# A Strassen-Winograd MLP in a hybrid decoder step: the second layer's seven products in another order, with other first steps and longer load leads

## The chip, the cores and the metric

The kernel runs on one core of a Trainium2 chip. A core has five engines that work side by side, each on its own list of instructions and strictly in the order of that list: TensorE (PE, products), VectorE (DVE), ScalarE (ACT), GpSimd (POOL) and SyncE (SP, which here only issues DMAs). Engines wait for one another through semaphores. The metric is the device time of one execution in microseconds; lower is better.

## The reference

One step of a hybrid decoder layer: attention and a state-space mixer, then a squared-ReLU MLP between RMSNorms. The change touches the second product of the MLP alone and what stands at its two ends:

```python
def rmsnorm(x, g):
    xf = x.astype(jnp.float32)
    y = xf * lax.rsqrt(jnp.mean(xf * xf, axis=-1, keepdims=True) + EPS)
    return (y * g.astype(jnp.float32)).astype(x.dtype)
...
    u = jax.nn.relu(rmsnorm(h, norm2_g) @ w_up)
    return h + (u * u) @ w_down
```

A last rmsnorm gives y. The model width is 1024, the MLP's 4096; there are 1024 prompt positions (without the meta tokens) and 32 of the running samples, 1056 columns (TM) in all. Everything is float32.

## The kernel before

**Numbers.** Each float32 operand is split into a high part in fp32r (a cast on ACT) and a low part (a subtraction on DVE), and each product of blocks is made as three: high by high, high by low, low by high (`three`). For weights, `split_w` (L1194 to L1198) does this into six rooms, used in turn: two each of whi, wlo and a third name (w7x in the up layer, w7y in the down layer). A room is free again when PE has ended the step that used it.

**MLP by seven products.** Both layers cut their matrices in two halves each way and use the Strassen-Winograd scheme, in which seven products of half size take the place of eight. The columns' halves have 528 columns (TH), a quarter 264 (TQ). The up layer runs over 16 pairs p of output blocks and, for each, over products j in the order 5, 1, 2, 6, 7, 4, 3 (1 and 2 of the first six pairs are done ahead); a product is 24 matmuls of 128x264. `run_up` copies sums from PSUM on ACT (s, L1243), adds on DVE, applies relu and square, and POOL writes the seven activation sums that the down layer needs to DRAM, `u7[k]`, one array for each k (L1316, L1317; k is the pair that made it). A pair's weights come in two loads (`load_up`, L1206), each into one of two rooms.

**Down layer.** `ORDER` gives the order of its products; the first six run as `down`, 16 steps k each. `step_down` (L1375) does one step: 24 matmuls into eight PSUM banks (two named c, three g, three b), all sums of a scheme added up in the banks. At k = 15 DVE adds the eight banks to a quarter of the residual h (L1386); `INTO` says which. The next product cannot write a bank until that addition has read it. The activation of a step is loaded into `tr` (L1493, 264 KB), cast (L1495) and split (L1496) into `ts`. The weights come from loads of 256 KB (wdr), with sums in place for some products: product 5 takes S = x + z (L1505), product 3 x - (S - R) with R (`Rd`) loaded there (L1510, L1511), product 1 R, 6 the new S, 7 R - x (L1519), 4 a block as it is. Weights are made two steps ahead of their use.

**First steps.** So that PE need not stop between the layers, `EARLY` = 3 steps of product 5 are loaded, summed and split in rooms of the up layer during its last pair (`load_first`, `sum_first`, `split_first`). The other rooms of the down layer are only opened behind it.

**End.** Product 2 has its own loop, over quarters and half the output blocks, with its weights (w2, from `wdq`) and activations (`tsq`, `tk`, from `trq`) prepared three ahead. `final` makes the last norm of a quarter of the columns: squares on ACT (L1529), their sums on DVE (q, down to `ac`), a product with ones on PE to add across partitions, x to -1/2 on POOL (L311, `rs`), a diagonal matrix `dg` (L1547), a product of that with ones to spread it, and the scaling of h (L1556). It is written as a generator, and each `next` between steps lets it do one piece.

A scheduler may move independent instructions of an engine past one another; what it did is shown below, as lists of the built programs.

Of the kernel before, what the change touches and what calls it, by code (L numbers as in the profile page):

```python
# [191 lines left out]
def body(ctx: ExitStack, tc: tile.TileContext, xT, xm, win, wdt, wo, wu, wd, ck, cv, sc, st, sT, vec, consts,  # L192
# [1011 lines left out]
    def load_up(p, n, early):  # L1204
        r = (pu if n or early else wring).tile([128, 8, 128], F32, name=f"wraw{n}", tag="wraw2" if n or early else "wraw", bufs=2)
        SP.dma_start(out=r, in_=wu[p + 16 * n])  # L1206
        raws[p, n] = r

    def prep_up(p, j, first):

        if first:
# [4 lines left out]
        if (p, 1) in raws:
            a21, a22 = raws[p, 1][:, 0:4], raws[p, 1][:, 4:8]
        tt = DVE.tensor_tensor
        if j == 5:
            S_[p] = pu.tile([128, 4, 128], F32, name="S", tag="S", bufs=2)  # L1220
            tt(out=S_[p], in0=a21, in1=a22, op=ALU.add)
        elif j == 6:
            tt(out=S_[p], in0=S_[p], in1=a11, op=ALU.subtract)
        elif j == 7:
            tt(out=a21, in0=a11, in1=a21, op=ALU.subtract)
# [116 lines left out]
    def load_first(k, part):  # L1342

        if k < 2 and part == "z":
            early["r", k] = raw_tile()
            early["w", k] = early["r", k][:, 0:4], early["r", k][:, 4:8]
        elif k == 2:
            early["w", k] = early["r", 0][:, 4:8], early["r", 1][:, 4:8]
        if part == "a":
            early["a", k] = pu.tile([128, 2, TQ], F32, name="x5", tag="s3" if k == 2 else "s1", bufs=1 if k == 2 else 2).rearrange("p c t -> p (c t)")  # L1350
            SP.dma_start(out=early["a", k], in_=u7[k][:, SLOT[5]])
        else:
            SP.dma_start(out=early["w", k][0], in_=wd[k, :, 1])
            SP.dma_start(out=early["w", k][1], in_=wd[k + 16, :, 1])

    def sum_first(k):
        x, z = early["w", k]
        DVE.tensor_tensor(out=x, in0=x, in1=z, op=ALU.add)
        Sv[k] = flat(x)

    def split_first(k):
        if k != 1:
            early["t"] = pu.tile([128, 4, TH], F32R, name="t5", tag="u" if k else "x", bufs=2)
        t, a = early["t"][:, 2 * (k % 2):2 * (k % 2) + 2], early["a", k]
        w = split_w(pu, "w7x", early["w", k][0])
# [112 lines left out]
    sr_s = ctx.enter_context(ExitStack())
    srp = sr_s.enter_context(pool("srp", side="right"))
    R = srp.tile([128, 16, 512], F32, name="Rd")  # L1480
    S = srp.tile([128, 16, 512], F32, name="Sd")
# [8 lines left out]
    def acts(j, k, a=0, w=TH):  # L1490

        x = dn.tile([128, TH], F32, name="tr", tag="tr", bufs=3)[:, :w]
        SP.dma_start(out=x, in_=u7[k][:, SLOT[j], a:a + w])  # L1493
        t = dn.tile([128, 2, TH], F32R, name="ts", tag="ts", bufs=3)[:, :, :w]
        ACT.copy(out=t[:, 0], in_=x)  # L1495
        DVE.tensor_tensor(out=t[:, 1], in0=x, in1=f(t[:, 0]), op=ALU.subtract)  # L1496
        return t

    def weights_down(j, k):
        tt = DVE.tensor_tensor  # L1500
        s, r = Sv.get(k, S[:, k]), R[:, k]
        shaped = lambda a: a.rearrange("p (m q) -> p m q", m=4)
        if j == 5:
            x, z = block(k, 1, 0), block(k, 1, 1)
            tt(out=s, in0=flat(x), in1=flat(z), op=ALU.add)  # L1505
            return shaped(s)
        if j == 3:
            SP.dma_start(out=shaped(r), in_=wd[k, :, 0])
            x = block(k, 0, 1)
            tt(out=s, in0=s, in1=r, op=ALU.subtract)  # L1510
            tt(out=flat(x), in0=flat(x), in1=s, op=ALU.subtract)  # L1511
            return x
        if j == 1:
            return shaped(r)
        if j == 6:
            return shaped(s)
        if j == 7:
            x = block(k, 1, 0)
            tt(out=flat(x), in0=r, in1=flat(x), op=ALU.subtract)  # L1519
            return x  # L1520
        return block(k, 1 if j == 4 else 0, 1)
# [170 lines left out]
```

## Time and profile before

| | |
|---|---|
| median of 3 timed runs | 1173.1 us (1171.42 to 1176.45) |
| the profiled execution: time | 1180.33 us |
| its span | 1178.6 us |
| mean granted TensorE clock | 0.981 |
| down layer, first step of product 5 to last step of the step loop | 816.5 to 1107.4 us |

The profile is of one execution. "Idle before" in brackets is how long an engine stood still ahead of an instruction, with what released it. The page divides the span into 40 slices of 29.5 us; here are PE's and the DMA's busy tenths and the clock:

```profile
PE   8999989999999998999999999998899999999996
...
PEclk9999999999999999999999999999999999999898
DMA  8311110111466477656552534336999433665373
```

### The profile page before, as it was taken

What the parts mean: (1) busy time and instruction counts of PE and PEld (TensorE: products, weight loads), DVE (VectorE), ACT (ScalarE), POOL (GpSimd) and SP (SyncE); (2) the same over time, 40 slices, a digit from 0 to 9 for tenths busy, and PEclk for the clock granted to TensorE, in tenths of its full rate; (3) what the DMA queues carried; (4) which work ended last, traced back from release to release, by engine and by line L of the source; (5) the groups of instructions that cost most, each with busy time, mean ns of one, the idle gap of its engine ahead of it and who ended that gap; (6) DMA issues with size and microseconds to landing.
All of it is one profiled execution on the core that took longest, in us unless ns stands there. A gap on an engine that the chain in (4) does not pass through costs nothing.

```text
span 1178.6 us, 21734 instructions
## 1 busy us (share of the span) xinstructions
PE 1130.9 (96%) x8393; PEld 1088.9 (92%) x8393; DVE 840.2 (71%) x1634; ACT 558.3 (47%) x1176; POOL 240.1 (20%) x258
## 2 busy tenths in 40 slices
PE   8999989999999998999999999998899999999996
PEld 6899978889888897999999999998899999999996
DVE  7665888996689955988777777775687654746583
ACT  7312556665576646854434444443334333444351
POOL 4632343634435454210000000000000000000000
PEclk9999999999999999999999999999999999999898
DMA  8311110111466477656552534336999433665373
GB/s 286 112 37 37 37 37 18 37 38 53 132 209 202 128 233 224 200 181 225 189 182 106 180 117 154 147 120 220 317 289 295 135 93 94 181 183 148 114 238 102
DMA packets 87448, 177.64 MB, mean 151 GB/s; under 512 B 11028, under 2 KB 37556, under 8 KB 85296
## 3 DMA queue, kind: packets, MB, share of 16 engines
q1 hardware_dynamic: 80288, 141.44, 39.7%
q0 software_dynamic: 6224, 33.74, 7.1%
q8 instruction: 66, 1.08, 0.4%
q10 hardware_dynamic: 832, 1.07, 0.3%
q14 instruction: 38, 0.31, 0.1%
HBM read 125.49 MB, written 50.72 MB: 150 GB/s over the span
## 4 chain that ended last, share of the span: by engine, by line
PE 61%; DVE 14%; DMA 10%; issue 6%; ACT 4%; POOL 1%; SPq 1%; DVEq 0%; POOLq 0%; ACTq 0%
PE g L202 34%; PE b L202 14%; PE c L202 7%; PE s L202 2%; DMA wdr<-in_wd 2%; PE o L202 1%; DMA trq<-u 1%; DVE bc L512 1%; DVE p L638 1%; DMA hb<-hd 1%; DMA Rd<-in_wd 1%; DMA tr<-u 1%; DVE Qs L671 1%; DMA wdq<-in_wd 1%; DMA hb<-in_xm 1%
## 5 line engine op out<-in xcount | busy, mean ns | idle before, releaser
L202 PE MATMUL g<-acth,wlo 128*128 128x384 f32 (+2 forms) x624 | 193.9, 331 | 4.5 <-DVE hb L918 3.7
L202 PE MATMUL g<-acth,whi 128*128 128x384 f32 (+2 forms) x624 | 195.8, 335 | 1.5 <-DVE hb L918 1.4
L202 PE MATMUL g<-actl,whi 128*128 128x384 f32 (+2 forms) x528 | 175.1, 332 | 1.0 <-DVE actl L397 1.0
L1495 ACT CAST ts<-tr 128x528 fp32r<-128x528 f32 x93 | 58.9, 633 | 141.3 <-PE b L202 112.2
L202 PEld LDWEIGHTS g<-acth,wlo 128*128 128x128 f32 x624 | 117.5, 192 | 8.0 <-issue 3.5
L1496 DVE TENSOR_TENSOR ts<-tr,ts 128x528 fp32r<-128x528 f32 x93 | 65.6, 707 | 79.2 <-ACT ts L1495 79.1
L202 PEld LDWEIGHTS g<-acth,whi 128*128 128x128 f32 x624 | 116.7, 191 | 5.1 <-issue 3.6
L202 PEld LDWEIGHTS g<-actl,whi 128*128 128x128 f32 x528 | 101.1, 192 | 3.6 <-DVE actl L397 2.5
L311 POOL TENSOR_TENSOR rs<-rs,nhalf 128x3 f32<-128x3 f32 x10 | 11.1, 1114 | 347.3 <-DVE rs L310 347.3
L1243 ACT COPY s<-g 128x264 f32<-128x264 f32 x90 | 34.0, 379 | 71.4 <-PE g L202 70.2
L1248 DVE TENSOR_TENSOR u<-b,s 128x264 f32<-128x264 f32 x64 | 27.5, 431 | 26.5 <-PE b L202 14.8
L1316 POOL DMA_DIRECT2D u<-u x16 | 8.5, 532 | 180.9 <-ACT u L1259 149.1
L225 POOL TENSOR_TENSOR wlo<-wraw,whi 128x1024 fp32r<-128x1024 f32 (+1 forms) x18 | 41.9, 2328 | 16.3 <-ACT whi L224 16.2
L1253 ACT ACTIVATE u<-u 128x528 f32<-128x528 f32 x42 | 27.1, 646 | 28.6 <-DVE u L1252 28.6
L202 PE MATMUL g<-ts,w7y 128*128 128x264 f32 x279 | 40.1, 290 | 0.0
L202 PE MATMUL b<-ts,wlo 128*128 128x264 f32 x279 | 39.9, 289 | 0.0
L202 PE MATMUL g<-ts,wlo 128*128 128x264 f32 x279 | 39.7, 288 | 0.0
L202 PE MATMUL b<-ts,w7y 128*128 128x264 f32 x279 | 39.6, 287 | 0.0
L202 PE MATMUL g<-ts,whi 128*128 128x264 f32 x279 | 39.2, 285 | 0.0
L202 PE MATMUL b<-ts,whi 128*128 128x264 f32 x279 | 38.6, 283 | 0.0
L202 PEld LDWEIGHTS g<-ts,w7y 128*128 128x128 f32 x279 | 37.1, 193 | 0.0
L202 PEld LDWEIGHTS b<-ts,wlo 128*128 128x128 f32 x279 | 36.9, 193 | 0.0
(550 smaller groups left out, 3358.5 us busy)
## 6 DMA issues: line engine op xcount, KB each, us to landing
tr<-u SPq DMA_DIRECT2D x93, 264.0 KB, 2.8
wraw<-in_wu SPq DMA_DIRECT2D x38, 512.0 KB, 3.9
wdr<-in_wd SPq DMA_DIRECT2D x74, 256.0 KB, 4.4
u<-t POOLq DMA_DIRECT2D x16, 1056.0 KB, 5.5
wraw<-in_win SPq DMA_DIRECT2D x16, 512.0 KB, 3.7
u<-u POOLq DMA_DIRECT2D x10, 792.0 KB, 3.6
wraw<-in_wo SPq DMA_DIRECT2D x24, 256.0 KB, 3.2
h<-he SPq DMA_DIRECT2D x16, 264.0 KB, 4.4
```

Source lines behind the costliest of these rows:

```text
L202: PE.matmul(out, lhsT=a, rhs=b, start=start, stop=stop, skip_group_check=on)
L225: eng.tensor_tensor(out=lo[:, k], in0=raw[:, k], in1=f(hi[:, k]), op=ALU.subtract)
L311: POOL.tensor_tensor(out=out, in0=out, in1=nhalf[:out.shape[0], :w], op=ALU.pow)
L512: DVE.scalar_tensor_tensor(out=acc, in0=cb[:, j:j + CL], scalar=cw_(j), in1=acc, op0=ALU.mult, op1=ALU.add)
L638: DVE.tensor_tensor_reduce(out=s_out, in0=ps, in1=mask, scale=-scale, scalar=nsink, op0=ALU.add, op1=ALU.min, accum_out=nm)
L671: DVE.tensor_tensor(out=Q[oth, g, :, :rows], in0=src, in1=f(Q[own, g, :, :rows]), op=ALU.subtract)
L1243: ACT.copy(out=s[:, c], in_=ps[c][:, :TQ])
L1248: DVE.tensor_tensor(out=out[:, c], in0=ps[c][:, :TQ], in1=s[:, c], op=ALU.add)
L1253: ACT.activation(out=x, in_=x, func=AF.Square)
L1316: POOL.dma_start(out=u7[p][:, 4 + a:7], in_=u[:, a:3])
L1495: ACT.copy(out=t[:, 0], in_=x)
L1496: DVE.tensor_tensor(out=t[:, 1], in0=x, in1=f(t[:, 0]), op=ALU.subtract)
```

## The change

It does five things.

1. The first six products of the down layer are run in the order 1, 6, 7, 4, 5, 3 in place of 5, 3, 1, 6, 7, 4; 2 stays last. So each weight sum is made where it is first needed: R is loaded in product 1, S made in product 6 from two loads and R, 5 takes S + R, 3 a block minus S. R and S are separate tiles for each k now.
2. Four steps in place of three are prepared ahead, of product 1 in place of 5: their weights are blocks as loaded, in two rooms of the last two pairs' weights, and the four activations go into the place of operand b11.
3. Up layer: `load_up` issues the loads of pairs one pair further ahead in the code, as far as the rooms allow.
4. Down layer: a step's loads are issued by `fetch_down`, up to three steps ahead of `prep_down`, which does the sums and splits; wdr has 10 rooms in place of 6, tr 5 in place of 3.
5. `final` adds each half of the squares by itself before the two are joined, and its pieces for c = 2 and 3 are begun in product 3 (k = 2, 4, 6) in place of 4; the loads of h move to k = 6, 8, 10, 12 of products 1, 6, 7, 4.

```diff
+    groups = [(p, (0,)) for p in range(NPRE)] + [(p, (0, 1)) for p in range(16)]
...
         if first:
-            load_up(p, 0, j == 1 and p < 2)
-            if j == 5:
-                load_up(p, 1, False)
+            load_up(g + 2)
+            if g == len(groups) - 1:
+                load_first((0, 1))
...
-    ORDER = (5, 3, 1, 6, 7, 4, 2)
+    ORDER = (1, 6, 7, 4, 5, 3, 2)
-    EARLY = 3
+    EARLY = 4
...
+    def load_first(ks):
+
+        raw = raw_tile()
+        for n, k in enumerate(ks):
+            SP.dma_start(out=raw[:, 4 * n:4 * n + 4], in_=wd[k, :, 0])
+            Rv[k] = raw[:, 4 * n:4 * n + 4]
+
+    def acts_first():
+        early["a"] = xa.tile([128, 4, TH], F32, name="x1", tag="xb11h")
+        for k in range(EARLY):
+            SP.dma_start(out=early["a"][:, k], in_=u7[k][:, SLOT[1]])
...
-                mm(dps[q][:, :TQ], w[:, a, m, :], t[:, b, two(c)], j in (5, 1) and k == 0 and n == 0, k == 15 and n == 2, j not in (5, 1))
+                mm(dps[q][:, :TQ], w[:, a, m, :], t[:, b, two(c)], j in (1, 5) and k == 0 and n == 0, k == 15 and n == 2, j not in (1, 5))
...
-            if j == 1:
-                load_first(0, "z")
-            elif j == 2:
-                load_first(0, "a")
-                load_first(1, "z")
+            if j == 2:
+                acts_first()
             elif j == 6:
-                load_first(1, "a")
-                sum_first(0)
-            elif j == 7:
+                load_first((2, 3))
+            elif j == 4:
                 split_first(0)
-                sum_first(1)
-                load_first(2, "z")
-            elif j == 4:
-                load_first(2, "a")
                 split_first(1)
             elif j == 3:
-                sum_first(2)
                 split_first(2)
+                split_first(3)
...
+    def fetch_down(i):
+
+        j, k = down[i]
+        if j == 1:
+            SP.dma_start(out=Rv[k], in_=wd[k, :, 0])
+            ws = []
+        else:
+            ws = [block(k, *b) for b in {6: ((1, 0), (1, 1)), 7: ((1, 0),), 4: ((1, 1),), 5: (), 3: ((0, 1),)}[j]]
+        x = dn.tile([128, TH], F32, name="tr", tag="tr", bufs=5)
+        SP.dma_start(out=x, in_=u7[k][:, SLOT[j]])
+        got[i] = ws, x
+
+    def prep_down(i):
+
+        j, k = down[i]
+        ws, x = got.pop(i)
+        r, s = flat(Rv[k]), flat(Sv[k])
+        tt = DVE.tensor_tensor
+        if j == 1:
+            w = Rv[k]
+        elif j == 6:
+            tt(out=s, in0=flat(ws[0]), in1=flat(ws[1]), op=ALU.add)
+            tt(out=s, in0=s, in1=r, op=ALU.subtract)
+            w = Sv[k]
+        elif j == 5:
+            w = dn.tile([128, 4, 128], F32, name="wdr", tag="wdr", bufs=10)
+            tt(out=flat(w), in0=s, in1=r, op=ALU.add)
...
-        for n in (4, 2):
-            DVE.tensor_tensor(out=q2[:, 0:n], in0=q2[:, 0:n], in1=q2[:, n:2 * n], op=ALU.add)
-            yield
-        DVE.tensor_tensor(out=acc, in0=q2[:, 0], in1=q2[:, 1], op=ALU.add)
+            for w in (2, 1):
+                DVE.tensor_tensor(out=q2[:, n:n + w], in0=q2[:, n:n + w], in1=q2[:, n + w:n + 2 * w], op=ALU.add)
+                yield
+        DVE.tensor_tensor(out=acc, in0=q2[:, 0], in1=q2[:, 4], op=ALU.add)
...
-        if k in (4, 6, 8, 10) and j in (5, 3, 1, 4):
+        if k in (6, 8, 10, 12) and j in (1, 6, 7, 4):
...
-        if j == 4 and k in (2, 4, 6, 8, 10):
+        if j == 3 and k in (2, 4, 6):
             for x in finals:
                 next(x)
...
-        for x in finals[:1] if i < 15 else finals[1:2] if i < 22 else finals[1:]:
+        for x in finals[:1] if i < 4 else finals:
```

In the lists that follow each row is an instruction with its line, what it writes and what it reads; lines behind L1360 are some four higher in the changed kernel.

**ACT, from the last pair of the up layer on.** In the kernel before, x_ are the activations of the early steps (L1366 their cast), s_9144 the copy that the next product of the last pair waits for:

```order
L1196 CAST wlo<-wraw 128x512
L1366 CAST t_9147<-x_9082 128x528
L1196 CAST w7x<-wraw 128x512
L1243 COPY s_9144<-g 128x264
L1253 ACTIVATE u<-u 128x528
L1366 CAST t_9147<-x_9117 128x528
L1243 COPY s_9144<-g 128x264
```

In the changed kernel (the cast is L1370, the copy L1254, the square L1264):

```order
L1196 CAST wlo<-wraw 128x512
L1370 CAST t_9178<-x_9082 128x528
L1196 CAST w7x<-wraw 128x512
L1370 CAST t_9178<-x_9082 128x528
L1370 CAST t_9216<-x_9082 128x528
L1264 ACTIVATE u<-u 128x528
L1254 COPY s_9144<-g 128x264
L1370 CAST t_9216<-x_9082 128x528
L1254 COPY s_9144<-g 128x264
```

Two more activation casts and the square stand ahead of the first copy of s_9144, and a fourth cast ahead of the second. The first steps that are not early follow on the same engine, behind the last square of u. Before:

```order
L1495 CAST ts<-tr 128x528 x3
L1196 CAST wlo<-Sd 128x512
L1196 CAST w7y<-Sd 128x512
L1196 CAST whi<-Sd 128x512
L1495 CAST ts<-tr 128x528
```

Now, with R of steps 4 to 9 as Rd_9389 down to Rd_9384:

```order
L1196 CAST whi<-Rd_9388 128x512
L1196 CAST wlo<-Rd_9387 128x512
L1196 CAST whi<-Rd_9385 128x512
L1196 CAST w7y<-Rd_9389 128x512
L1196 CAST w7y<-Rd_9386 128x512
L1196 CAST wlo<-Rd_9384 128x512
L1520 CAST ts<-tr 128x528 x4
L1196 CAST w7y<-Rd_9383 128x512
```

Six weight casts stand ahead of the first activation cast, the last of them into the wlo room of the fourth early step.

**DVE, at the first boundary of the down layer.** Before, from product 5 to 3, the h additions (L1386) stand behind S - R (L1510) and the next activation:

```order
L1197 TENSOR_TENSOR wlo<-wdr,wlo 128x512
L1511 TENSOR_TENSOR wdr<-wdr,Sd 128x512
L1510 TENSOR_TENSOR Sd<-Sd,Rd 128x512
L1496 TENSOR_TENSOR ts<-tr,ts 128x528
L1386 TENSOR_TENSOR h<-h,c 128x264 x2
L1386 TENSOR_TENSOR h<-h,g 128x264 x3
L1386 TENSOR_TENSOR h<-h,b 128x264 x3
```

Now, from product 1 to 6 (Sd_9399 is the S of step 9, Sd_9393 that of step 3; the additions are L1390):

```order
L1521 TENSOR_TENSOR ts<-tr,ts 128x528
L1197 TENSOR_TENSOR w7y<-Sd_9393,w7y 128x512
L1506 TENSOR_TENSOR Sd_9399<-wdr 128x512
L1507 TENSOR_TENSOR Sd_9399<-Sd_9399,Rd_9384 128x512
L1390 TENSOR_TENSOR h<-h,c 128x264
L1521 TENSOR_TENSOR ts<-tr,ts 128x528
L1390 TENSOR_TENSOR h<-h,c 128x264
```

The wait for R ahead of the additions is not there; two sums for the tenth step of product 6 stand in that place.

**PE, at the end of the step loop.** Before, ac_12174 and ac_12177 being the sums of c = 2 and 3:

```order
L202 MATMUL b<-ts,whi 128x264 x9
L202 MATMUL b<-ones,ac_12174 128x1 x3
L202 MATMUL b<-dg_12815,ones 128x128 x3
L202 MATMUL b<-ones,ac_12177 128x1 x3
L202 MATMUL c<-tsq,w_0_12668 128x264 x2
L202 MATMUL g<-tsq,w_0_12668 128x264 x2
```

Now:

```order
L202 MATMUL b<-ts,whi 128x264 x9
L202 MATMUL b<-ones,ac_12235 128x1 x3
L202 MATMUL b<-ones,ac_12238 128x1 x3
L202 MATMUL c<-tsq,w_0_12724 128x264 x2
L202 MATMUL g<-tsq,w_0_12724 128x264 x2
L202 MATMUL b<-dg_12967,ones 128x128 x2
L202 MATMUL c<-tsq,w_0_12724 128x264 x4
```

Both products with ones come first, and the product with dg stands behind the first products of the last loop. On DVE these rows are behind the last h additions now:

```order
L1533 TENSOR_TENSOR q_12234<-q_12234 128x264
L1535 TENSOR_TENSOR ac_12235<-q_12234 128x264
L1533 TENSOR_TENSOR q_12237<-q_12237 128x528
L310 TENSOR_SCALAR rs_12966<-b 128x3
L1533 TENSOR_TENSOR q_12237<-q_12237 128x264
L1548 TENSOR_TENSOR dg_12967<-cs,rs_12966 128x384
L1535 TENSOR_TENSOR ac_12238<-q_12237 128x264
L1638 TENSOR_TENSOR w_0_12724<-wdq,w_0_12724 128x512
```

The sums that give both ac were done before that point in the kernel before; here they, rs and dg stand one behind another, and the first split of a weight of product 2 (L1638) behind them.

More of the change, by code (lines that the diff above doesn't have):

```diff
@@ L1142, in operand @@
     def operand(p, name):
-        OP[name] = [p.tile([128, 4, TH], F32R, name=f"x{name}{q}") for q in "hl"]
+        OP[name] = [p.tile([128, 4, TH], F32R, name=f"x{name}{q}", tag=f"x{name}{q}") for q in "hl"]
         return OP[name]
@@ L1202, in body, with load_up @@
     raws, S_, wts, chain, s_, us = {}, {}, {}, {}, {}, {}
[L1204 to L1207, printed above, removed]
+    groups = [(p, (0,)) for p in range(NPRE)] + [(p, (0, 1)) for p in range(16)]
+    loaded = [0]
+    def load_up(upto):
+        while loaded[0] < min(upto, len(groups)):
+            g = loaded[0]
+            p, ns = groups[g]
+            loaded[0] += 1
+            for n in ns:
+                own = n or g < 2
+                r = (pu if own else wring).tile([128, 8, 128], F32, name=f"wraw{n}", tag="wraw2" if own else "wraw", bufs=2)
+                SP.dma_start(out=r, in_=wu[p + 16 * n])
+                raws[g, n] = r
     def prep_up(p, j, first):
+        g = p if p < NPRE and j in (1, 2) else NPRE + p
         if first:
-            load_up(p, 0, j == 1 and p < 2)
-            if j == 5:
-                load_up(p, 1, False)
-        a11, a12 = raws[p, 0][:, 0:4], raws[p, 0][:, 4:8]
-        if (p, 1) in raws:
-            a21, a22 = raws[p, 1][:, 0:4], raws[p, 1][:, 4:8]
+            load_up(g + 2)
+            if g == len(groups) - 1:
+                load_first((0, 1))
+        a11, a12 = raws[g, 0][:, 0:4], raws[g, 0][:, 4:8]
+        if g >= NPRE:
+            a21, a22 = raws[g, 1][:, 0:4], raws[g, 1][:, 4:8]
         tt = DVE.tensor_tensor
@@ L1330, in prepare @@
             prepared[0] += 1
-    ORDER = (5, 3, 1, 6, 7, 4, 2)
+    ORDER = (1, 6, 7, 4, 5, 3, 2)
     SLOT = {5: 0, 6: 1, 7: 2, 4: 3, 1: 4, 2: 5, 3: 6}
     down = [(j, k) for j in ORDER[:-1] for k in range(16)]
-    EARLY = 3
-    early, Sv = {}, {}
+    EARLY = 4
+    early, Rv = {}, {}
     def flat(a):
         return a.rearrange("p m q -> p (m q)")
[L1342 to L1359, printed above, removed]
+    def load_first(ks):
[7 more added lines that the diff above has]
+            SP.dma_start(out=early["a"][:, k], in_=u7[k][:, SLOT[1]])
     def split_first(k):
[L1362 to L1365, printed above, removed]
+        if k % 2 == 0:
+            early["t"] = pu.tile([128, 4, TH], F32R, name="t1", tag="u" if k else "x", bufs=2)
+        t, a = early["t"][:, 2 * (k % 2):2 * (k % 2) + 2], early["a"][:, k]
+        w = split_w(pu, "w7x", Rv[k])
         ACT.copy(out=t[:, 0], in_=a)
@@ L1376, in step_down @@
         j, k = down[i]
-        if k == 0 and j in (5, 1):
+        if k == 0 and j in (1, 5):
             dps[:] = [bank(t) for t in BANKS]
@@ L1474, in body @@
     up_s.close()
-    dn_s = ctx.enter_context(ExitStack())
+    sr_s, dn_s = (ctx.enter_context(ExitStack()) for _ in range(2))
+    srp = sr_s.enter_context(pool("srp", side="right"))
     dn = dn_s.enter_context(pool("dn", side="right"))
     hpool = ctx.enter_context(pool("hpool"))
[L1478 to L1481, printed above, removed]
+    Rv.update({k: srp.tile([128, 4, 128], F32, name=f"Rd{k}") for k in range(15, EARLY - 1, -1)})
@@ L1482, in body @@
+    Sv = {k: srp.tile([128, 4, 128], F32, name=f"Sd{k}") for k in range(16)}
     h = hpool.tile([128, 8, TM], F32, name="h")
-    ready = {}
+    got, ready = {}, {}
     def block(k, mh, kh):
-        r = dn.tile([128, 4, 128], F32, name="wdr", tag="wdr", bufs=6)
+        r = dn.tile([128, 4, 128], F32, name="wdr", tag="wdr", bufs=10)
         SP.dma_start(out=r, in_=wd[k + 16 * kh, :, mh])
         return r
[L1490 to L1494, printed above, removed]
+    def fetch_down(i):
[8 more added lines that the diff above has]
+        got[i] = ws, x
@@ new lines, in prep_down @@
+    def prep_down(i):
[12 more added lines that the diff above has]
+            tt(out=flat(w), in0=s, in1=r, op=ALU.add)
+        else:
+            w = ws[0]
+            if j == 7:
+                tt(out=flat(w), in0=r, in1=flat(w), op=ALU.subtract)
+            elif j == 3:
+                tt(out=flat(w), in0=flat(w), in1=s, op=ALU.subtract)
+        t = dn.tile([128, 2, TH], F32R, name="ts", tag="ts", bufs=3)
+        w = split_w(dn, "w7y", w)
@@ L1495, in acts @@
         ACT.copy(out=t[:, 0], in_=x)
         DVE.tensor_tensor(out=t[:, 1], in0=x, in1=f(t[:, 0]), op=ALU.subtract)
[L1497 to L1521, printed above, removed]
+        ready[i] = w, t
@@ L1548, in final @@
                           in1=rs.unsqueeze(2).broadcast_to([128, 3, 128]), op=ALU.mult)
-        yield
+        for _ in range(4):
+            yield
         ps = bank(tag)
@@ L1552, in final @@
             mm(ps[:, a:a + 128], ones, dg[:, q, :], True, True)
-        for _ in range(4):
+        for _ in range(3):
             yield
@@ L1567, in body @@
         while done < min(i + 3, len(down)):
-            jj, kk = down[done]
-            ready[done] = split_w(dn, "w7y", weights_down(jj, kk)), acts(jj, kk)
+            while fetched < min(done + 3, len(down)):
+                fetch_down(fetched)
+                fetched += 1
+            prep_down(done)
             done += 1
-        if k in (4, 6, 8, 10) and j in (5, 3, 1, 4):
+        if k in (6, 8, 10, 12) and j in (1, 6, 7, 4):
             mh, th = INTO[j]
-            m = 4 * mh + k // 2 - 2
+            m = 4 * mh + k // 2 - 3
             SP.dma_start(out=h[:, m, TH * th:TH * th + TH], in_=he[:, m, TH * th:TH * th + TH])
-        if j == 4 and k in (2, 4, 6, 8, 10):
+        if j == 3 and k in (2, 4, 6):
             for x in finals:
```

4 lines of the change are left out of this document (2 added, 2 removed).

## The prediction

> **What bounds the kernel now.** The page comes first, to see which engine is full.
>
> ```profile
> PE 1130.9 (96%) x8393; PEld 1088.9 (92%) x8393; DVE 840.2 (71%) x1634; ACT 558.3 (47%) x1176; POOL 240.1 (20%) x258
> ```
>
> TensorE is busy for 96% of the span, and the change alters neither the number nor the shape of its products. So the time can only come from the places where PE stands still, and from what those stops do to its clock. The view of waits, for PE alone from 500 us on (the relu layer and all behind it), lists the stops: who waited, what released it, total, times, longest. The largest and the smallest:
>
> ```profile
> PE g L202 <- ACT s L1243: 5.7, 3, 3.6
> ...
> PE c L202 <- DVE ts L1496: 0.2, 1, 0.2
> ```
>
> The PE timeline (start, time, products, and in brackets the idle time ahead) gives each its place. I call them A to F.
>
> ```profile
> 583.74 0.39 PE L202 MATMUL g<-xt3h,wlo 128*128 128x264 f32 x1 [1.93 <-ACT s L1243]
> 806.26 0.59 PE L202 MATMUL g<-xt3h,wlo 128*128 128x264 f32 x1 [3.56 <-ACT s L1243]
> 828.59 0.76 PE L202 MATMUL c<-ts,wlo 128*128 128x264 f32 x4 [3.13 <-ACT wlo L1196]
> 870.59 1.49 PE L202 MATMUL c<-ts,w7y 128*128 128x264 f32 x6 [2.06 <-DVE h L1386]
> 1110.04 1.65 PE L202 MATMUL b<-dg,ones 128*128 128x128 f32 x6 [1.81 <-DVE dg L1547]
> ```
>
> A (583.74) is early in the up layer, B (806.26) in its last pair. C (828.59) follows the three early steps of the down layer. D (870.59) is the boundary from product 5 to 3, F (1110.04) the end of the six products of the step loop. E is the 0.2 us above; behind F lie three of under 0.6 us and one of 1.93 in the tail, which the change leaves. Each stop costs more than its idle time, as the windows behind them show (PE busy, PEld, DVE, ACT, POOL, granted clock, DMA share, GB/s).
>
> ```profile
> 829.90:833.30 3.40, 3.40 (x18) 3.40 (x17) 1.00 (x2) 0.00 (x0) 0.00 (x0) 0.51 0.84 262
> 870.80:874.20 3.40, 3.40 (x17) 3.40 (x17) 3.40 (x9) 0.00 (x0) 0.00 (x0) 0.50 0.85 254
> 1143.10:1146.50 3.40, 3.40 (x30) 3.40 (x29) 3.37 (x9) 1.22 (x4) 0.00 (x0) 1.00 0.59 159
> 940.00:1100.00 160.00, 160.00 (x1311) 160.00 (x1310) 88.70 (x147) 65.78 (x111) 0.00 (x0) 1.00 0.50 143
> ```
>
> Behind C and D the clock is 0.51 and 0.50 for 3.4 us, and PE does 17 or 18 products there in place of some 28. Behind an idle of 0.30 us, the one before 1143, it stays at 1.00. From 940 to 1100 nothing waits: 160 us, all busy. A step of 24 products takes 160 x 24/1311 = 2.93 us there. The price of a drop comes from the starts of the step behind the slow one.
>
> ```profile
> 833.06 0.99 PE L202 MATMUL c<-ts,w7y 128*128 128x264 f32 x6
> 875.12 0.91 PE L202 MATMUL c<-ts,whi 128*128 128x264 f32 x6
> ```
>
> The steps behind C and D take 833.06 - 828.59 = 4.47 and 875.12 - 870.59 = 4.53 us. So C costs 3.13 + 1.54 = 4.7 us and D 2.06 + 1.60 = 3.7.
>
> [...]
>
> **The change part by part.** *Loads further ahead, up layer.* A's copy on ACT stands behind a chain that begins with a pair's load, late on DVE:
>
> ```profile
> 579.61 0.69 DVE L1225 TENSOR_TENSOR wraw<-wraw,wraw 128x512 f32<-128x512 f32 x1 [2.70 <-DMA wraw<-in_wu]
> ```
>
> The pair loads still have two rooms of each kind, and their place in SP's queue, each behind the same DVE subtraction that frees its room, is the old one up to the last pair. So A stays: 0. If its load did start earlier, 1.93 and a drop of some 1.6, 3.5 together, would be the most to gain.
>
> *B, the last pair.* Now PE waits for an s copy on ACT, behind a cast of product 5's weight sum, behind its load.
>
> ```profile
> 796.42 7.97 DMA wraw<-in_wd
> ...
> 804.51 0.70 DVE wraw L1358
> ...
> 805.84 0.38 ACT s L1243
> ```
>
> The load lands at 804.4, beside a write of t. The change drops the sum but puts three casts of x (x_0 to x_2) and a square (L1264) ahead of that copy. The four x loads, 264 KB each, issue when PE ends the products before, 0.2 us behind the load above at the earliest, beside the same write and two weight loads.
>
> ```profile
> u<-t POOLq DMA_DIRECT2D x16, 1056.0 KB, 5.5
> 815.90:830.00 14.10, 10.97 (x90) 10.75 (x89) 8.78 (x15) 4.28 (x7) 1.06 (x2) 0.99 0.99 343
> ```
>
> That is 1056 + 4 x 264 + 2 x 256 = 2624 KB. At the 343 GB/s of a full stretch it takes 7.8 us, from 795.6 to 803.4 or, with a slow start as here, 804.5. Then come a cast, the square and the copy, some 0.63 + 0.65 + 0.38: PE goes on between 805 and 806.3. I take B at 0, with -1.5 (a late x) to +1.5.
>
> *C, the first prepared step.* Of before, the chain is this:
>
> ```profile
> 815.94 9.95 DMA tr<-u
> ...
> 827.20 0.69 DVE Sd L1505
> 827.92 0.63 ACT wlo L1196
> ```
>
> A step's activation landed late, and its casts and the weight sums stood one behind another. Product 1 needs no sum, a fourth early step gives PE 2.93 us more, and the activation's load is issued when the early steps begin, some 10 us of transfer ahead of its use. But ACT now has six weight casts ahead of the first activation cast, and the sixth (wlo of k=9) takes a room that frees only when PE has ended the fourth early step. So PE must wait: about 0.2 for the signal, one weight cast, one activation cast.
>
> ```profile
> L1495 ACT CAST ts<-tr 128x528 fp32r<-128x528 f32 x90 | 57.0, 633 | 135.1 <-PE b L202 112.2 <-issue 12.7 <-DMA tr<-u 6.1
> L1196 ACT CAST wlo<-Sd 128x512 fp32r<-128x512 f32 x9 | 5.6, 617 | 3.0 <-DVE Sd L1505 2.9
> ```
>
> That is 0.2 + 0.62 + 0.63 = 1.4 us; DVE's subtraction behind the cast is covered by the first products, hi by hi. Does 1.4 drop the clock? Idle of 0.30 did not, 1.81 to 3.56 did. 1.4 is nearer to 1.81, so I take a drop of 1.6: C costs 3.0 instead of 4.7, **gain 1.7**. Without the drop the gain is 3.3; if the load is late too, none.
>
> *D and E.* In product 3 DVE had to wait for Rd just ahead of the h additions that free PE's banks.
>
> ```profile
> 868.79 0.69 DVE L1510 TENSOR_TENSOR Sd<-Sd,Rd 128x512 f32<-128x512 f32 x1 [0.98 <-DMA Rd<-in_wd]
> 870.02 0.76 DVE L1386 TENSOR_TENSOR h<-h,c 128x264 f32<-128x264 f32 x2
> ...
> 830.00:850.00 20.00, 20.00 (x153) 20.00 (x153) 13.87 (x22) 7.56 (x13) 0.00 (x0) 0.92 0.93 312
> 890.00:912.00 22.00, 22.00 (x182) 22.00 (x181) 16.45 (x27) 10.22 (x17) 0.00 (x0) 1.00 0.88 281
> ...
> wdr<-in_wd SPq DMA_DIRECT2D x74, 256.0 KB, 4.4
> ...
> tr<-u SPq DMA_DIRECT2D x93, 264.0 KB, 2.8
> ```
>
> The DMA share is 0.88 to 0.93 around it, because products 5 and 3 each load 256 + 256 + 264 = 776 KB a step, back to back. Now only product 6 loads so much; 1 and 5 take 520 and 264 KB, 7, 4 and 3 take 520. So 5 to 3 comes late, in a quiet stretch with 0.50 of the DMA: D goes, **gain 3.7**, E 0.2. What is late next is the boundary 1 to 6. There DVE has the two sums for k = 9 of product 6 before its h additions, and their loads stand in SP's queue behind an activation whose room frees only with DVE's split of step 15's. That work can start when PE has ended step 12, 8.8 us ahead of the end of step 15; a cast and a subtraction (1.3), three or four issues and the load's median of 4.4, and two sums (1.4) take 8 to 8.8. So DVE is ready 0 to 0.8 us ahead of PE. I take 0 as loss; it would be up to D's whole 3.7.
>
> *F, the end.* Of final's norms, the sums for the second sample half (c = 2, 3) were made inside product 4, since both lay ready. Now the last product of the loop is 3, which writes one of the halves that they need, so both columns of sums stand behind its last additions, on DVE in series.
>
> ```profile
> 1107.43 0.80 PE L202 MATMUL b<-ones,ac 128*128 128x1 f32 x6
> ...
> 1118.93 0.89 PE L202 MATMUL c<-tsq,w 128*128 128x264 f32 x6
> ...
> 1106.92 1.15 DVE L1386 TENSOR_TENSOR h<-h,b 128x264 f32<-128x264 f32 x3
> ...
> 1109.09 1.07 ACT L1529 ACTIVATE q<-h 128x1056 f32<-128x1056 f32 x1
> ...
> 1109.42 0.56 DVE L1547 TENSOR_TENSOR dg<-cs,rs 128x384 f32<-128x384 f32 x1 [0.99 <-POOL rs L311]
> 1109.90 0.70 DVE L1597 TENSOR_TENSOR q<-q 128x528 f32<-128x528 f32 x1
> ...
> 1110.10:1113.40 3.30, 3.30 (x15) 3.30 (x16) 2.17 (x5) 3.30 (x10) 0.00 (x0) 0.50 0.00 0
> ```
>
> Before, PE starts the ones product at T' = 1107.43 and the fourth weight of product 2 at T' + 11.50, with 36 products between. After, from the end T of the last step: its additions end at T + 0.6 as now; a Square (1.07), whose first half DVE reads as soon as it is there, and the additions of the halves (0.70, and some 0.4 for each of 264, by 0.38 for an addition to h) put the first ac at T + 2.3, the first rs at T + 3.3, POOL's pow (0.99, by the wait ahead of dg) and dg at T + 4.9, the second ac at T + 5.3. The second ones products and the first products with tsq follow, then, behind a split of the weight and one of tsq, dg's at T + 6.5, and the fourth weight at about T + 12.6. The clock is 0.50 in it, before (1110.10) as after. **Loss 1.1 to 1.4**, taken 1.3, bounds 0 (PE's slow stretch merely shifts) and 3. The last tail (1165 on) I leave at 0 +- 0.7, since y's pieces for c = 2, 3 are stored in the 45 us of product 2 as before, only later.
>
> **The sum.** Gains 1.7 + 3.7 + 0.2, losses 1.3: 4.3 us. The profiled execution took 1180.3 us, span 1178.6; it would take about 1176.0. The median of the three timed runs is 1173.1, 7.2 less, so I carry the difference over: **1168.8 us**, a gain of 0.37%. A measurement of this kernel can tell about 0.5% from no change, 5.9 us.
>
> **The rivals.** *More is gained.* C's 1.4 us does not drop the clock (+1.6), B's loads land early (+1), F costs nothing more (+1.3). One of the three gives 5.3 to 5.9, two 6.6 to 7.2, all 8.2: 1165 to 1167. [...]
>
> *The boundary comes back.* DVE is late at 1 to 6 by 1 to 2 us, which takes back 2 to 3.7 (with a drop). Result 1171 to 1172.5. For it speaks the order on DVE, against it the DMA's load: from 816 to 912 some 29 MB passed (343 GB/s for 14.1 us, some 297 for 82), and from 809 to the end of product 6 they are 12 x 256 + 28 x 264 + 32 x 256 of the steps, 8 x 264 of h and 1848 KB of writes, 23 MB, in a longer time.
>
> [...]
>
> *Slower: the end of the loop.* The pow was twice as long once (least, median, most):
>
> ```profile
> L311 POOL TENSOR_TENSOR rs<-rs,nhalf x10: 848/881/1915, 18.9 to 1168.9; 128x3 f32<-128x3 f32 x10
> ```
>
> If DVE's serial chain of two norms holds PE until T + 7.0 with such a pow, all 36 products run at half clock (8.8 us), and the next 3.4 us too (1.7 lost): the fourth weight comes at T + 15.8, with 1.7 more behind, 6.0 over before. It decides from 5.6 on, where it eats the other gains: 1173 to 1174, above 1179 only if the loads of product 2, whose rooms free later, slip as well. DVE's many short links speak for it; the median of 0.88 speaks against it.
>
> *The change does not do what it says:* loads for pairs stay bound by rooms (A stays), which the forecast holds already.
>
> **How the numbers follow.** [...] Faster by over 0.5% takes the second case: 0.34. Slower by over 0.5% takes most of the last: 0.07. Within: 0.59. The likeliest is 1168.8. The range leaves out the top of the gains and the far end of the slower case: 1163.5 (gain 8.2, and 1.5 of B) to 1174.5.
>
> **What would show it.** A right: 1.9 us near 584 again. B: PE waits between 2 and 5 us for an s copy at 806, behind the cast of x_2. C: one idle of about 1.4 us after four early steps, released by ACT's activation cast, and the clock behind it tells the 1.6. D: no wait for h at the boundaries, and above all none at 1 to 6, the windows there at 1.00. F: two ones products, then tsq, and about 12.6 us from the last step's end to the fourth weight. Wrong would be a new wait for a load in product 6, a clock of 0.50 in more than one window of the boundaries, or an F of 15 us.

## The result: slower by 0.4%, and the profile after

The changed kernel takes 1178.3 us (median of 14 runs, 1176.1 to 1184.7), the kernel before 1172.5 in as many runs (1168.8 to 1178.6). The ratio is 1.0043, with an interval of 1.0028 to 1.0058. The forecast was 1168.8, with 1163.5 to 1174.5; the time lies above that range.

The profiled execution of the changed kernel took 1178.03 us, at its median, span 1176.2. That is 2.4 us *less* than the span of before that the prediction read, although the timed runs say 5.8 more. So two things want an answer: where the changed kernel stands still, and what is wrong with that comparison. Here is PE's line of the page after, and the three largest rows of the view of PE's waits from 500 us on:

```profile
PE 1127.4 (96%) x8393; PEld 1086.4 (92%) x8393; DVE 851.3 (72%) x1656; ACT 557.2 (47%) x1176; POOL 241.7 (21%) x258
```

```profile
PE g L202 <- ACT s L1254: 6.6, 3, 4.2
PE b L202 <- DVE ac L1535: 4.3, 2, 2.3
PE c L202 <- DVE h L1390: 3.6, 1, 3.6
```

The PE timeline of after gives the places (idle time ahead in brackets):

```profile
584.31 0.39 PE L202 MATMUL g<-xt3h,wlo 128*128 128x264 f32 x1 [1.93 <-ACT s L1254]
...
806.77 0.59 PE L202 MATMUL g<-xt3h,wlo 128*128 128x264 f32 x1 [4.24 <-ACT s L1254]
...
831.00 0.51 PE L202 MATMUL c<-ts,w7y 128*128 128x264 f32 x2 [1.28 <-ACT ts L1520]
...
870.02 1.90 PE L202 MATMUL c<-ts,w7y 128*128 128x264 f32 x6 [3.58 <-DVE h L1390]
...
1107.78 0.83 PE L202 MATMUL b<-ones,ac 128*128 128x1 f32 x6 [2.08 <-DVE ac L1535]
1110.88 1.44 PE L202 MATMUL b<-ones,ac 128*128 128x1 f32 x6 [2.27 <-DVE ac L1535]
...
1118.56 0.90 PE L202 MATMUL c<-tsq,w 128*128 128x264 f32 x6
```

A (584) is as it was. B has grown to 4.24. C is 1.28. D is gone from the boundary 5 to 3, but at 870.02, the boundary 1 to 6, PE waits 3.58 us for an h addition. The last step ends at 1105.70, and the fourth weight of product 2 starts 12.86 us behind it (before, from the same point: 11.33). Behind B and behind the boundary the clock drops; the windows (granted clock third from the right):

```profile
806.90:810.30 3.40, 3.40 (x16) 3.40 (x17) 1.86 (x4) 1.53 (x4) 0.00 (x0) 0.50 0.00 0
870.10:873.50 3.40, 3.40 (x16) 3.22 (x17) 3.40 (x10) 0.00 (x0) 0.00 (x0) 0.56 0.89 313
```

### The profile page after: what moved, and what is told of

Its sections match the earlier page's. It is cut to its first block, busy times and chain, and to the rows that moved or that the text cites. A ratio compares the mean times of both kernels' runs of the same rounds, so it can differ in the third digit from the quotient of the medians.

```text
span 1176.2 us, 21740 instructions
## 1 busy us (share of the span) xinstructions
PE 1127.4 (96%) x8393; PEld 1086.4 (92%) x8393; DVE 851.3 (72%) x1656; ACT 557.2 (47%) x1176; POOL 241.7 (21%) x258
## 3 DMA queue, kind: packets, MB, share of 16 engines
q8 instruction: 66, 1.08, 0.4%
## 4 chain that ended last, share of the span: by engine, by line
PE 68%; DVE 13%; DMA 7%; issue 5%; ACT 4%; POOL 2%; SPq 0%; POOLq 0%; DVEq 0%; ACTq 0%
PE g L202 37%; PE b L202 17%; PE c L202 9%; PE s L202 2%; DMA wdr<-in_wd 2%; PE o L202 1%; DMA hb<-hd 1%; DMA he<-hb 1%; DVE bc L512 1%; DVE p L638 1%; DVE Qs L671 1%; ACT p L640 1%; DVE xs L512 1%; PE pt L706 1%; DVE actl L397 1%
## 5 line engine op out<-in xcount | busy, mean ns | idle before, releaser
L1254 ACT COPY s<-g 128x264 f32<-128x264 f32 x90 | 33.9, 378 | 70.0 <-PE g L202 68.8
L1264 ACT ACTIVATE u<-u 128x528 f32<-128x528 f32 x42 | 27.1, 646 | 31.7 <-DVE u L1263 31.7
L202 PE MATMUL b<-ts,wlo 128*128 128x264 f32 x270 | 37.3, 282 | 0.0
L202 PEld LDWEIGHTS b<-ts,w7y 128*128 128x128 f32 x279 | 36.2, 188 | 0.0
```

What stands on the lines that cost most here:

```text
L202: PE.matmul(out, lhsT=a, rhs=b, start=start, stop=stop, skip_group_check=on)
L1254: ACT.copy(out=s[:, c], in_=ps[c][:, :TQ])
L1264: ACT.activation(out=x, in_=x, func=AF.Square)
```

## The experiments

**The kernel before, twice more (b2, b3).** No edit; only a profile of each.

> The kernel before, profiled once more. Its first profile took 1180.33 us, 7.8 over the median of its 14 runs (1172.5); the profile of after took 1178.03, at its median (1178.3). Theory one (the first profile of before was a high draw, and its stops C and D, which depend on when loads land, are smaller in common runs): 1170 to 1174 us, and of C 3.13 and D 2.06 us idle at least one under half. Theory two (the stops are the same in each run, the 7.8 us lie elsewhere): 1170 to 1174 us with C and D within 0.5 us of those. A time above 1178 again would tell nothing.

> As b2, a third profile of the kernel before, since one draw can mislead again. Theory one: C + D under 3 us idle and 1170 to 1174 us. Theory two: C + D 4.5 to 5.5 us idle.

Measured: 1172.98 and 1169.43 us. PE's stops of b2, then of b3:

```profile
802.55 0.40 PE L202 MATMUL g<-xt3h,wlo 128*128 128x264 f32 x1 [1.64 <-ACT s L1243]
823.09 0.75 PE L202 MATMUL c<-ts,wlo 128*128 128x264 f32 x4 [2.72 <-ACT wlo L1196]
865.24 0.98 PE L202 MATMUL c<-ts,w7y 128*128 128x264 f32 x6 [2.21 <-DVE h L1386]
```

```profile
802.12 0.59 PE L202 MATMUL g<-xt3h,wlo 128*128 128x264 f32 x1 [2.52 <-ACT s L1243]
824.04 0.76 PE L202 MATMUL c<-ts,wlo 128*128 128x264 f32 x4 [2.56 <-ACT wlo L1196]
864.11 0.97 PE L202 MATMUL c<-ts,w7y 128*128 128x264 f32 x6 [1.65 <-DVE h L1386]
```

C + D is 4.9 and 4.2 us idle, 5.2 in the first profile: the stops are there in each run, as theory two says (b3 a little under its bound), and theory one falls. What differs is B (1.64 and 2.52, not 3.56) and the clock behind the stops. The windows behind D of b2, then C and D of b3:

```profile
865.30:868.70 3.40, 3.40 (x28) 3.40 (x29) 3.40 (x10) 0.21 (x1) 0.00 (x0) 1.00 0.89 278
```

```profile
824.10:827.50 3.40, 3.40 (x28) 3.40 (x29) 2.25 (x4) 1.30 (x3) 0.00 (x0) 1.00 0.99 322
864.20:867.50 3.30, 3.30 (x28) 3.30 (x28) 3.30 (x10) 0.13 (x1) 0.00 (x0) 1.00 0.81 239
```

After idle times of 2.21, 2.56 and 1.65 us the clock stayed at 1.00, with 28 products where the first profile had 17 or 18. The first profile had a drop behind all five stops, A, B, C, D and F, at some 1.6 us each (1.54 and 1.60 at C and D, taken for the others too); b2 has one (behind C) and a short one (F), b3 two (B and F). So the first profile, from which the prediction took its prices, was an unusually slow execution.

**Rooms of product 2 (room).** Tiles that are kept for later are made later, so that the first loads' rooms lie elsewhere:

```diff
-    kept2 = [w2p.tile([128, 2, TQ], F32R, name=f"tk{k}") for k in range(16)]
+    kept2 = []
...
     def acts_last(c, k):
+        if c and not kept2:
+            kept2.extend(w2p.tile([128, 2, TQ], F32R, name=f"tk{n}") for n in range(16))
```

> After, with the tiles kept for the second half of product 2 made later, so that the rooms of its weights and activations lie where R and S were and its first loads need not wait for the last step of product 3. In after's profile these loads issue at T + 0.03 (1105.73) and PE stands still 4.35 us in two pieces behind T, fourth weight at T + 12.86. If the late loads set F: loads 6 to 16 us earlier, fourth weight at T + 11 to 12, 1 to 2 us faster than after (1176.5 to 1177.5). If DVE's chain of two norms sets it: loads earlier, fourth weight still at T + 12.4 to 12.9, time as after within 0.5 us.

Measured: 1178.8 us, ratio to before 1.0043 (1.0026 to 1.0061), as the changed kernel. The loads of the first weights issued at 1086.9 to 1100.9, with the last step's end at 1108.4, and the fourth weight still began 12.85 us behind it. The late loads are real and set nothing; DVE's chain does.

**Sums of product 6 on POOL (poolsum).**

```diff
-            tt(out=s, in0=flat(ws[0]), in1=flat(ws[1]), op=ALU.add)
-            tt(out=s, in0=s, in1=r, op=ALU.subtract)
+            POOL.tensor_tensor(out=s, in0=flat(ws[0]), in1=flat(ws[1]), op=ALU.add)
+            POOL.tensor_tensor(out=s, in0=s, in1=r, op=ALU.subtract)
```

> After, with the two sums that make S in product 6 on POOL, which has nothing to do there, instead of DVE. In after's profile PE stands still 3.58 us at the boundary 1 to 6 for an h addition that stands on DVE behind a sum that waits 1.61 us for its load. If that order is the cause: no stop at 1 to 6 (under 0.5 us), its clock at 1.00, 4 to 5.5 us faster than after (1173 to 1174.5). If the load itself is what PE lacks: the stop moves to the first steps of product 6, released by a cast of S, and the gain is under 2 us.

Measured: 1182.8 us (1.0083, 1.0063 to 1.0103), 4.5 more than the changed kernel. The stop at 1 to 6 fell to 0.72 and 1.01 us, but two new ones stand further on in product 6, 1.14 and 4.14 us. The groups by line show why:

```profile
L1506 POOL TENSOR_TENSOR Sd<-wdr 128x512 f32<-128x512 f32 x16 | 27.8, 1735 | 20.6 <-DMA wdr<-in_wd 20.6
L1507 POOL TENSOR_TENSOR Sd<-Sd,Rd 128x512 f32<-128x512 f32 x12 | 19.1, 1592 | 0.9
```

Two sums take 3.3 us on POOL, and a step of PE 2.93. And DVE, whose splits release the two new stops, became slow as well: while POOL ran these sums, from 841.3 to 895.3 us, DVE's splits took some 1.77 us each, ahead of that and behind it 0.69. In the changed kernel they take 0.68 there. The splits of w7y in poolsum (least, median, most, in ns):

```profile
L1197 DVE TENSOR_TENSOR w7y<-Sd,w7y x6: 677/1771/1777, 851.9 to 905.5; 128x512 fp32r<-128x512 f32 x6
```

So neither theory is tested by this run, and it tells little of the list on DVE. Runs hold and light had to.

**An earlier room for the first activations (xroom).**

```diff
-        early["a"] = xa.tile([128, 4, TH], F32, name="x1", tag="xb11h")
+        early["a"] = xb.tile([128, 4, TH], F32, name="x1", tag="xt1h")
...
-            if j == 2:
+            if j == 1:
                 acts_first()
```

> After, with the four activations of the early steps in the room of operand t1 (free when PE ends product 5 of the last pair) instead of b11 (free one product later), so that their loads go out some 3 us earlier, ahead of the write of t. In after's profiles the first of these loads takes 6.7 and 7.1 us beside that write, and PE stands still 4.24 and 4.49 us at B. If the late loads are the cause: B under 1 us and its clock at 1.00, 4 to 6 us faster than after (1172.5 to 1174.5). If only the casts' place on ACT is: B 2 to 3.5 us, gain 1 to 2.

Measured: 1171.5 us, 0.998 of before (0.9967 to 0.9994), 6.8 less than the changed kernel and a little more than forecast. The stop B is gone. ACT in the changed kernel, then in xroom:

```profile
803.52 0.63 ACT L1370 CAST t<-x 128x528 fp32r<-128x528 f32 x1 [5.88 <-DMA x<-u]
804.05 0.61 ACT L1196 CAST w7x<-wraw 128x512 fp32r<-128x512 f32 x1
804.57 1.33 ACT L1370 CAST t<-x 128x528 fp32r<-128x528 f32 x2
805.81 0.64 ACT L1264 ACTIVATE u<-u 128x528 f32<-128x528 f32 x1
806.36 0.36 ACT L1254 COPY s<-g 128x264 f32<-128x264 f32 x1
```

```profile
795.21 0.64 ACT L1370 CAST t<-x 128x528 fp32r<-128x528 f32 x1 [1.09 <-DMA x<-u]
...
799.96 0.37 ACT L1254 COPY s<-g 128x264 f32<-128x264 f32 x1
```

In the changed kernel ACT waits 5.88 us for the first x; then two more casts of x, a weight cast, the square and the copy follow before PE can go on. In xroom the loads issue from 792.3 on, ahead of the write of t, and land in 2.8 to 5.3 us in place of 6.6 to 7.6. The casts are still there, and PE does not stop: the late loads are the cause.

**The norms behind product 2's first steps (gate).** Rooms as in room, and:

```diff
+        if gate:
+            for n in (4, 0):
+                ACT.copy(out=q2[:, n, 0:1], in_=f(tq[gate][:, 0, 0:1]))
         for n in (4, 0):
             ACT.activation(out=q2[:, n:n + 4], in_=hc[:, n:n + 4], func=AF.Square)
...
-    finals = [final(2, "b"), final(3, "b")]
+    finals = [final(2, "b", 4), final(3, "b", 6)]
...
-        if j == 3 and k in (2, 4, 6):
-            for x in finals:
-                next(x)
...
-        for x in finals[:1] if i < 4 else finals:
+        for x in () if i < 1 else finals[:1] if i < 3 else finals:
```

> After, with the rooms as in the run room, and with final's squares for c = 2 and 3 held back until the activations of steps 4 and 6 of product 2 are there (by a copy of one column that the squares overwrite), so that DVE's two norms no longer stand between the last step and product 2. T to the fourth weight is 12.9 us in after's profile, 11.5 in before's, and 4.4 of it are work. If the norms' place is what F costs: 5 to 6.5 us, no half clock there, 6 to 7.5 faster than after (1171 to 1172.5). If the splits of product 2's first weights, behind the same h additions, are: 9 to 11 us, gain 2 to 4.

Measured: 1173.5 us, 0.9996 of before (0.9984 to 1.0008), 4.8 under the changed kernel, where 6 to 7.5 were expected. PE at the end of the loop:

```profile
1100.91 1.25 PE L202 MATMUL b<-ts,whi 128*128 128x264 f32 x9
1102.00 0.40 PE L202 MATMUL c<-tsq,w 128*128 128x264 f32 x2
1102.24 0.28 PE L202 MATMUL g<-tsq,w 128*128 128x264 f32 x1
1103.63 0.76 PE L202 MATMUL c<-tsq,w 128*128 128x264 f32 x4 [1.10 <-DVE tsq L1648]
```

PE goes over to product 2 with 1.10 us of idle time and no drop; the fourth weight starts some 5.6 us behind the last step, in place of 12.86. Of the 7.3 us won there some 2.5 do not show in the median: the norms' products stand in product 2 now, and three waits of 0.25 to 0.50 us for its activations appear around 1111 to 1116 (1.15 us together). Where the rest goes was not followed.

**The lead alone, both ways (lead0, blead).** lead0 is the changed kernel without it (6 and 3 rooms for wdr and tr, as before), blead the kernel before with it (its loads go into a fetch_down of its own, 10 and 5 rooms):

```diff
-            while fetched < min(done + 3, len(down)):
+            while fetched < min(done + 1, len(down)):
```

> After, with the down layer's loads issued together with the sums and splits as in before (no lead of three steps), 6 rooms for wdr and 3 for tr. At the boundary 1 to 6 DVE still does sums some nine steps ahead in its list. If the lead is what fills the DMA engines there (0.87 of them before 870) and makes the sums late: stop at 1 to 6 under 1.5 us, 2 to 4 us faster than after. If DVE's list alone is the cause: the stop stays 3 to 5 us, and the time is that of after within 1 us, or longer, since each load has less time.

> Before, with the lead alone: loads of the down layer three steps ahead, 10 rooms for wdr, 5 for tr; order, early steps and end as before. If longer leads help by themselves: D (1.65 and 2.21 us in the runs b3 and b2) goes and the time is 2 to 4 us under before (1169 to 1171.5). If the DMA engines are full at this place (0.9) and a lead cannot make up for that: D stays at 1.5 us or more, time within 1.5 us of before's.

Measured: lead0 1179.9 us (1.0049, 1.0031 to 1.0067), with 3.85 us at 1 to 6: as its second theory has it. blead 1175.6 us, 1.0021 of before (1.0006 to 1.0036). There neither theory holds: D goes, as the first says, and yet the time is 2.7 us longer: in its one profile C takes 4.89 us where b2 and b3 have 2.72 and 2.56, and a stop of 2.03 appears at 3 to 1. In blead loads of later steps are issued ahead in the same queue. That these hold up the first activation was not tried apart.

**Product 6's sums held back (hold), and lighter (light).** hold makes the sums for k of 4 and more wait for product 1's additions; light leaves out one of the two blocks of product 6 and takes the other twice, so that a step loads 520 KB in place of 776 with the same work on DVE:

```diff
+            if k >= 4:
+                DVE.tensor_copy(out=s[:, 0:1], in_=h[:, 3, TH - 1:TH])
             tt(out=s, in0=flat(ws[0]), in1=flat(ws[1]), op=ALU.add)
```

```diff
-            ws = [block(k, *b) for b in {6: ((1, 0), (1, 1)), 7: ((1, 0),), 4: ((1, 1),), 5: (), 3: ((0, 1),)}[j]]
+            ws = [block(k, *b) for b in {6: ((1, 0),), 7: ((1, 0),), 4: ((1, 1),), 5: (), 3: ((0, 1),)}[j]]
...
-            tt(out=s, in0=flat(ws[0]), in1=flat(ws[1]), op=ALU.add)
+            tt(out=s, in0=flat(ws[0]), in1=flat(ws[0]), op=ALU.add)
```

> After, with the sums of product 6 for k of 4 and more held back until product 1's h additions are done (a one-column copy from h that the sums overwrite). In after's profiles DVE has the sums for k = 9 ahead of those additions, one waits 1.61 us for its load, and PE stands still 3.58, 3.49, 3.42, 3.85 us at 1 to 6 (after, room, xroom, lead0). If DVE's list is the cause of that stop: under 0.5 us there, 4 to 5 us faster than after (1173.5 to 1174.5). If the loads are what is short: the stop moves into product 6, released by a cast of S or ts, and the gain is under 2 us.

> After with one of product 6's two weight blocks left out (S is made from one block taken twice), so that product 6 loads 520 KB a step in place of 776, with the same DVE work. If the DMA engines' load around 1 to 6 (776 KB in 2.93 us is 271 GB/s) makes the sums late: stop there under 1 us, 3 to 5.5 us faster than after. If it is the order on DVE or the room of an activation, whatever the load: 2.5 us or more are left.

Measured: hold 1173.1 us (1.0003, 0.9986 to 1.0019), light 1173.7 us (1.0007, 0.9988 to 1.0027), 5.2 and 4.6 less than the changed kernel. In hold PE crosses the boundary without a stop; in light 0.41 us are left. PE of hold, the last weight's last banks of product 1 and the first of 6, then the one stop of light:

```profile
865.18 1.24 PE L202 MATMUL b<-ts,wlo 128*128 128x264 f32 x9
866.26 0.91 PE L202 MATMUL c<-ts,w7y 128*128 128x264 f32 x6
```

```profile
865.20 0.97 PE L202 MATMUL c<-ts,w7y 128*128 128x264 f32 x6 [0.41 <-DVE h L1390]
```

Either cures it: the stop needs both a list on DVE that has sums ahead of the additions, and loads that come late for these sums.

**Together (xgate, xgatehold).** The edits of xroom and gate, and these with hold.

> After with the changes of xroom (activations of the early steps in a room that is free earlier) and of gate (norms behind the first steps of product 2). They took 6.8 and 4.8 us off after's median and lie 290 us apart. If the two causes are independent: 1166 to 1168 us, 0.994 to 0.996 of before. If what the one saves is lost again behind it (a wait for loads that come no earlier): 1169 to 1171.

> xgate with the sums held back as in hold. If the boundary is a third independent cost: 4 to 5 us under xgate, 1161 to 1164 us, 0.99 of before. If sums that cannot run ahead make product 6 wait: at xgate's time or over.

Measured: xgate 1167.9 us, 0.9949 of before (0.9930 to 0.9968); xgatehold **1162.6 us**, 0.9914 of before (0.9887 to 0.9940), the fastest of all kernels here. xroom, gate and hold took 6.8, 4.8 and 5.2 us off the changed kernel, 16.8 together; in one kernel it is 15.7. So they are three costs that add up nearly whole. The largest of PE's stops that are left in xgatehold:

```profile
PE g L202 <- ACT s L1254: 2.9, 2, 2.1
PE c L202 <- DVE dg L1624: 1.9, 1, 1.9
PE c L202 <- DVE tsq L1650: 1.5, 2, 1.1
```

## Why the prediction was wrong

**What was right.** A stayed (1.93 again), and the loads ahead did nothing in the up layer. C was forecast at 1.4 us idle behind the sixth weight cast, and is 1.28, released by ACT's activation cast (0.08 of it between PE's last product and the weight cast, where the sum put 0.2 for the signal, the author's estimate, which no run shows); the drop of 1.6 us that the sum added to it did not come (clock 1.00). F was forecast at T + 12.6 for the fourth weight and is T + 12.86, 1.5 us more than before where 1.3 was put in; room and gate show that the cause is the one named, two norms in series on DVE.

**The step that failed first: D returns at 1 to 6.** It was given as a rival, and its loss taken at 0 in the sum, on a margin of 0 to 0.8 us. Measured are 3.58 us and, with them, a drop; the same place shows 3.49, 3.42, 3.85 and 3.57 in room, xroom, lead0 and xgate, and 2.03 in gate, each time with a drop (0.50 to 0.59). The working looked at the right place, but its list was short. The chain of the changed kernel and the timeline of its DVE:

```profile
860.41 5.06 DMA wdr<-in_wd
```

```profile
865.57 0.69 DVE L1506 TENSOR_TENSOR Sd<-wdr 128x512 f32<-128x512 f32 x1 [1.61 <-DMA wdr<-in_wd]
866.29 0.69 DVE L1507 TENSOR_TENSOR Sd<-Sd,Rd 128x512 f32<-128x512 f32 x1
866.90 0.70 DVE L1521 TENSOR_TENSOR ts<-tr,ts 128x528 fp32r<-128x528 f32 x1
867.52 0.68 DVE L1197 TENSOR_TENSOR w7y<-Sd,w7y 128x512 fp32r<-128x512 f32 x1
868.12 0.69 DVE L1506 TENSOR_TENSOR Sd<-wdr 128x512 f32<-128x512 f32 x1
868.84 0.69 DVE L1507 TENSOR_TENSOR Sd<-Sd,Rd 128x512 f32<-128x512 f32 x1
869.45 0.42 DVE L1390 TENSOR_TENSOR h<-h,c 128x264 f32<-128x264 f32 x1
```

The forecast counted two sums (1.4 us) between the load and the addition. It was one load earlier that came late, in 5.06 us where the median of 4.4 had been put in, and six instructions, 3.9 us, stood behind it. hold prices the whole at 5.2 us. That the DMA had less to do in this stretch than before (23 MB against 29) was the argument against this rival, and it averaged over a hundred us: from 850 to 866.4 the share is 0.87, as at the boundary of before (0.88 to 0.93), since loads for product 6 already fall into it; light, with 520 KB of them a step in place of 776, has 0.41 us left of the stop.

```profile
850.00:866.40 16.40, 16.40 (x135) 16.23 (x134) 12.90 (x21) 5.86 (x11) 0.00 (x0) 1.00 0.87 278
```

**The second: B at 0.** The forecast had all four x landed by 803.4 to 804.5, and behind the last of them a cast, the square and the copy, 1.66 us. Measured, the first x landed only at 803.4, and the last, issued at 799.2, took 6.6 us, to 805.8. So ACT could not do the casts one by one while the loads came in: two further casts and a weight cast fall behind the first landing too, and from 803.52 to the end of the copy ACT needs 3.2 us. B becomes 4.24, 4.2 to 5.6 in all seven runs that keep this order and room. Against 3.56 in the first profile that is little; against the 1.64 and 2.52 of b2 and b3 it is some 2.2 us and, each time, a drop. xroom takes the stop and the drop away, 6.8 us in all.

**The third: the base.** The gains were priced in one execution, 7.2 us over the median, and that difference was carried as a constant. b2 and b3 show that it was no constant but, for the most part, clock drops and B, in the very stops that were priced. C and D were put at 4.7 and 3.7 us, each with a drop; D costs 2.21 and 1.65 in b2 and b3, without one, and C there has a drop in b2 alone. So what the change could win was less than the 5.6 us of the sum, and what it made (4.24 and 3.58, both with a drop) more.

**The sum, from the rows.** The rest of b2's stops, from its view of PE's waits:

```profile
PE b L202 <- DVE dg L1547: 1.8, 1, 1.8
PE c L202 <- DVE ts L1496: 1.3, 2, 0.9
PE c L202 <- DVE tsq L1642: 0.8, 1, 0.8
```

Idle time of PE from B to the first weights of product 2: in b2 1.64 + 2.72 + 2.21 + 1.3 + 1.8 + 0.8 = 10.5, in b3 2.52 + 2.56 + 1.65 + 1.80 (F) = 8.5; after 4.24 + 1.28 + 3.58 + 2.08 + 2.27 = 13.5. That is 4.0 more than their mean, and with one to one and a half drops more (the changed kernel has three: B, the boundary, F) at 1.6 us each, an estimate of 5.6 to 6.4, beside 5.8 between the medians. How often which stop of the timed runs has a drop is not known, so the split of this last part stays open.

## What to carry to other kernels

A profile is one execution: where stops of two or three microseconds carry the sum, take the price from two or three profiles, and ask which of the stops' costs belong to that run alone. When work moves, write down everything that stands on the in-order engine between the late load and the instruction that PE waits for, and price the row, not the instruction that was moved. An engine's list that runs sums far ahead is no gift where loads are short: a wait there holds up whatever stands behind (1.61 us on DVE in the changed kernel, and 3.58 on PE), and a one-column copy that ties the early work to the urgent work bought 5.2 us in hold.

## What the runs showed of the hardware that was not expected

**The length of a stop of two microseconds does not decide whether the clock drops.** In the 14 profiles of this case the clock in the 3.4 us behind each of the 15 longest stops from 500 us on (3.42 us in xroom up to 5.6) read 0.50 to 0.64. For stops of 1.6 to 3.2 us that stand alone ahead of the tail, it read under 0.75 in 14 of 29, and 0.86 to 1.00 in the other 15. Behind the 1.28 us at C it read 1.00 in all ten kernels that have it; but behind two stops close together, of 0.72 and 1.01 us, in poolsum, it read 0.61. The same stop, A, in the first profile of before and in that of after:

```profile
583.90:587.40 3.50, 3.50 (x18) 3.50 (x18) 2.06 (x5) 1.45 (x4) 0.31 (x1) 0.53 0.83 285
```

```profile
584.40:587.80 3.40, 3.40 (x28) 3.40 (x29) 2.97 (x7) 1.66 (x5) 0.37 (x1) 1.00 0.80 268
```

Both stood still 1.93 us, and one did 18 products, the other 28. What else decides it, no run here shows.

**Four small loads beside a large write waited for it.** In the changed kernel the four x loads of 264 KB, issued 796.7 to 799.2 behind two weight loads of 256 KB in their own queue and beside a write of 1056 KB from another, took 6.6, 7.0 (median) and 7.6 us; issued one product earlier, ahead of those, they took 2.8 to 5.3 (xroom). From 799 to 801 us the write's queue moved 0.69 MB and the loads' queue 0.09; from 801 to 803.3 it was 0.11 and 0.63. So 0.69 of the write's 1.08 MB went in those two microseconds, and 0.99 of the loads' 1.61 MB behind it, from 801 to 806 us.

**DVE's splits were slow beside POOL's sums.** In poolsum a DVE split took some 1.77 us while POOL ran its sums, and 0.69 ahead of them and behind. DVE's additions to h, which read one operand from PSUM, stayed at 0.42 us for 264 columns beside the same sums.
